# MLP opening: eight weight blocks in buffers of their own, all twelve written ahead of the first product; early rows for the odd layer's output projection; a weight ring of nine

## The chip, the cores and the metric

The kernel runs on one core of a Trainium2 chip. The metric is the device time of one execution in microseconds (us), the median of three runs. In the profile the engines are PE (matrix multiply), DVE (vector), ACT (scalar), POOL (general) and SP, which issues the transfers.

## The reference

A trunk of two mixer layers, each followed by a squared-ReLU MLP, and a final normalisation. Input and output are 1024 tokens of 1024 channels in float32; the hidden width of an MLP is 4096.

```python
def sq_relu_mlp(h, w1, w2):
    u = jax.nn.relu(h @ w1)
    return (u * u) @ w2
...
def odd_mixer(h, w_in, ..., w_out):
    ...
    yc = dense_mla(qn, qr, kn, rope(kr), v)      # 8 heads, all keys, softmax
    yd = rglru_block(xr, xg, ...)                # recurrent branch
    return jnp.concatenate([yc, yd], axis=-1) @ w_out
```

Every layer is `x + layer(rmsnorm(x))`: even mixer (windowed attention beside a pooling branch), MLP 0, odd mixer, MLP 1, final norm.

## The kernel before, in words

Activations lie channel-major, 128 channels by 1024 tokens to a tile (`N2` = 512 is half the tokens). To keep float32 accuracy every operand of a product is split into a rounded high part and the rest: `split` is a cast, usually on ACT (L122), and a subtraction on DVE or POOL (L130). A product then takes three matrix multiplies, high by high, high by low, low by high (`mm3`, L185).

**The MLPs** use a seven-product scheme for 2x2 blocks. For each pair of hidden blocks `p` the first matrix gives the weight blocks A11, A12, A22 and the sums S1 to S4 (formed on POOL); the input gives B11 and B21 (the first half of the tokens) and t2, t3, T1, t4, B22, which mix both halves. One product (L378) is 12 matrix multiplies of 128x512: four channel blocks by three. `w_stream` is a generator that loads raw blocks (`raw`, 128x1024, 512 KB), splits the wanted block (`prep`, under high priority) and yields it; `Ahead` keeps some blocks of it made in advance, and `take` hands them out. The split blocks (`wb`) come from the ring of `W_BUFS` buffers tagged "w"; the other large tiles (`raw`, `hb` for split inputs, X) come from the pool `G` of 41.

An MLP **opens** with the pairs 0 to 5 (`NS` = 6), for which it runs A11·B11 (`head`, whose result ACT copies to `t1`, L396) and A12·B21 (`head2`, into the same PSUM tile, so it has to wait for that copy): 12 products that need only the first half of the tokens. Meanwhile the second half is finished: the sum of squares goes through PE (`ss`, L220), the reciprocal root through ACT and DVE, PE spreads it over the partitions (`rb`, L231), ACT copies it to `RB` (L235). Then `late` makes the mixed inputs, on DVE eight scaled halves (L1528), four differences (L1540), the t2, t3, T1 and t4 combinations (L1543 to L1555) and twenty splits with their casts on ACT. The **rest** of each opening pair needs those.

**The odd layer's end.** Eight heads of attention run in 128 steps `u`: scores, exponentials (ACT), their scaling (`e`, L1106, POOL), transposes (`ctp`, L1350) copied to `cpT` (ACT L1353, DVE L1354), and values (`cav`, L1124), which lag by `ODD_LAG` = 4 steps. The recurrent half `yd` is done long before. After the last step the output projection (`op`, L185) runs over two token halves `n` and eight blocks `m`, each with eight channel blocks `k`, the `yd` half (k 4 to 7) first. Its weights go through `fetch`: a raw ring of two, a transfer of 512 KB, a cast on ACT, a subtraction on POOL (`wl`, L130), both into the "w" ring. Its results close the layer's norm and open MLP 1, so the last of them and the first products of the MLP are interleaved.

The order on each engine is set by a scheduler that goes by priorities and free buffers when the program is built; at run time each engine works through its list in that order.

Of the kernel before, what the change touches and what calls it, by code (L numbers as in the profile page):

```python
# [10 lines left out]
F32R = mybir.dt.float32r  # L11
# [13 lines left out]
N2 = 512  # L25
# [21 lines left out]
class Trunk:  # L47
# [89 lines left out]
    def requests(self, ph):  # L137
        a = self.a
        if ph == "even":
            r = [(a["e_w_in"][i], S) for i in (4, 5, 0, 1, 2, 3)] + [(a["e_w_pool"], N2)]  # L140
            r += [(a["e_w_in"][i], S) for i in (9, 8, 7, 6)]
            r += [(a["e_w_out"][1][m], S, "act", "pool") for m in range(4)]
            return r + [(a["e_w_out"][0][m], S) for m in range(4)]
        if ph == "odd":
            idx = {"xr3": 6, "ckv": 2, "cq0": 0, "cq1": 1, "xg0": 7, "xg1": 8, "xg2": 9, "xg3": 10}
            late = {"kn": (a["w_uk"], N2), "qr": (a["w_uq_r"], N2), "qn": (a["w_uq_n"], S), "vn": (a["w_uv"], N2)}
            r = [(a["o_w_in"][i], S, "act" if i != 5 else "pool") for i in (3, 4, 5)]
            seen = set()
            for op in ODD_START:
                k = op[:-1]  # L150
                if k in seen:
                    continue
                seen.add(k)
                if k in idx:
                    r.append((a["o_w_in"][idx[k]], S, "pool"))
                elif k in late:
                    r.append(late[k])
            return r + [(a["o_w_out"][m], S, "act", "pool") for m in range(NC)] * 2
        if ph == "final":
            return []  # L160
        l = int(ph[-1])
        return [(a["w2"][l, f], S) for p in TAIL for f in pair(p)]
# [5 lines left out]
    def fetch(self, ahead):  # L168

        while self.wreq and len(self.wout) < ahead:  # L170
            src, n, *eng = self.wreq.pop(0)
            raw = self.wp.tile([P, S], F32, tag="raw", name=self.nm("raw"), bufs=RAW_BUFS)
            self.nc.sync.dma_start(raw[:, :n], src)
            h = self.wp.tile([P, S], F32R, tag="w", name=self.nm("wh"))
            l = self.wp.tile([P, S], F32R, tag="w", name=self.nm("wl"))
            self.split(h[:, :n], l[:, :n], raw[:, :n], *eng)
            self.wout.append((h, l))

# [93 lines left out]
    def block(self, tag, x, le="dve", neg=False):  # L272

        nc = self.nc
        w = self.wp.tile([P, S], F32R, tag="w", name=self.nm(tag)) if tag == "wb" else self.G(tag, F32R)
        h, l = w[:, :N2], w[:, N2:]
        if neg:
            nc.scalar.activation(h, x, AF.Copy, scale=-1.0)
# [11 lines left out]
    def w_stream(self, l, order, second, look=0):  # L290
# [23 lines left out]
            sums[p, b] = self.H2("sum", "sum")  # L314
            return sums[p, b]

        def prep(p, b):
            if b in ("A11", "A12", "A22"):
                x = blk(p, int(b[1]) - 1, int(b[2]) - 1)
            elif b == "S1":  # L320
# [12 lines left out]
            else:  # L333
# [6 lines left out]
                else:  # L340
                    x = sums[p, "S2"]
                    add(x, x, blk(p, 0, 1), op=ALU.add)
            return self.block("wb", x)

        uses = {"A11": (0,), "A12": (1,) if second else (0,), "A22": (1,), "S1": (0, 1) if second else (1,),
                "S2": (0, 1), "S3": (0,) if second else (0, 1), "S4": (0, 1)}
        for k, (p, b) in enumerate(order):
            for q, c in order[k:k + look + 1]:
                for i in uses[c]:
                    raw(q, i)  # L350
            with self.tc.high_priority():
                w = prep(p, b)
            yield w

    def first_stream(self, l):
# [7 lines left out]
    def mlp(self, l, nb, nxt, dram):  # L363
# [5 lines left out]
        stream = nb.stream  # L369
# [547 lines left out]
    def odd(self, nb, xs, nxt):  # L917
# [195 lines left out]
        def av(u):  # L1113
# [13 lines left out]
            if p % 2 == 1 and kk == 3:  # L1127
                if h % 2 == 0 and p == 1:
# [4 lines left out]
                nc.vector.tensor_tensor(yc[h // 2][r:r + 64, (p // 2) * N2:(p // 2 + 1) * N2], ACC[0][0:64],  # L1133
                                        tmp[0:64], op=ALU.add)

        prep = iter(())
        for u in range(4 * NS):
            i, kk = divmod(u, 4)
            h, p = steps[i]
            for op in ODD_STEP:  # L1140
# [11 lines left out]
                elif op == "V":  # L1152
                    av(u - ODD_LAG)
                elif op == "P":
                    if p == 0 and kk == 0 and 1 <= h < 7:
                        prep = prep_qk(h + 1)
                    next(prep, None)
            if p == 1 and kk == 3 and h < 7:
                VS[h + 1] = self.head_values(h + 1, Vn)
        Yh, Yl = [None] * 8, [None] * 8  # L1160
        for c in range(4):
            Yh[4 + c], Yl[4 + c] = self.G("yh", F32R), self.G("yl", F32R)
            for s in H2:
                self.split(Yh[4 + c][:, s], Yl[4 + c][:, s], yd[c][:, s], "act", "pool")
# [10 lines left out]
        for n in range(2):  # L1175
            for m0 in range(0, NC, 2):
                W = [self.weight(), self.weight()]
                grp = [(m0 + j, self.PS("op")) for j in range(2)]
                for part in range(2):
                    ks = order[4 * part:4 * part + 4]  # L1180
                    for m, ps in grp:
                        w = W[m - m0]
# [131 lines left out]

    def head_values(self, h, Vn):
        nc = self.nc
        VS = self.wp.tile([P, S], F32R, tag="w", name=self.nm("VS"))
        vv = VS.rearrange("p (b t d) -> p b t d", b=8, t=2)
        for i in range(4):
            src = Vn[i].rearrange("p (b h d) -> p b h d", b=2, h=8)[:, :, h, :]  # L1320
# [23 lines left out]
    def mla_transpose(self, pr, kk):  # L1344
        nc = self.nc
        tp = self.PB("ctp")
        for i in range(2):
            for j in range(2):
                kb = 2 * kk + i
                nc.tensor.transpose(tp[:, (2 * i + j) * P:(2 * i + j + 1) * P], pr[j][:, kb * P:(kb + 1) * P],  # L1350
                                    self.ident)
        pp = self.wp.tile([P, S], F32R, tag="w", name=self.nm("cpT"))
        nc.scalar.copy(pp[:, :N2], tp)  # L1353
        nc.vector.tensor_tensor(pp[:, N2:], tp, pp[:, :N2], op=ALU.subtract)  # L1354
        return pp
# [324 lines left out]
LOOK = 7  # L1680

G_BUFS = 41
W_BUFS = 8
RAW_BUFS = 2


# [125 lines left out]
```

## Time and profile before

| | |
|---|---|
| median of 3 runs | 2158.83 us (2158.75 to 2159.36) |
| profiled execution, device time | 2161.66 us |
| its span, first to last instruction | 2159.5 us |
| PE busy | 2051.3 us, 95% of the span |
| DVE / ACT / POOL busy | 1542.9 / 1065.0 / 823.2 us |
| mean granted PE clock | 0.987 |
| opening of MLP 0 / MLP 1, first product to fifteenth | 311 to 373 / 1484 to 1544 us |
| last steps of the odd attention | 1379 to 1403 us |

A timeline row reads: start, duration, engine, line, operation, output <- inputs, count, and in brackets the idle time before it on its engine with what ended that. Matrix multiplies overlap, so a row of 60 in 13.89 us means 0.2315 us for each.

### The profile page before, as it was taken

To read this page: it belongs to the slowest core of one execution; us is meant where nothing else is said; L and a number is where in the kernel's file an instruction comes from. 1 tells how busy PE (TensorE), PEld (TensorE's weight loads), DVE (VectorE), ACT (ScalarE), POOL (GpSimd) and SP (SyncE) were. 2 spreads that over 40 slices of the span, in tenths; PEclk is the share of its full clock that TensorE was granted. 3 is DMA by queue.
4 is the path that set the end of the run, shared out by engine and by line. 5 is a ranking of instruction groups with operands and counts; after the bars stand their busy time and mean duration, and the time that the engine had idled before them with its cause. 6 is when DMAs were issued, how large, how long until landed. Compare 5 with 4: busy or idle time off the path is not lost.

```text
span 2159.5 us, 27248 instructions
## 1 busy us (share of the span) xinstructions
PE 2051.3 (95%) x9600; PEld 1688.1 (78%) x9600; DVE 1542.9 (71%) x2365; ACT 1065.0 (49%) x1853; POOL 823.2 (38%) x635
## 2 busy tenths in 40 slices
PE   6989998999999999999997999999899999999997
PEld 5867776787777888888785898888678777788887
DVE  7688868765656877775898888717875655877964
ACT  5236645444544534340565777734645545544423
POOL 4133332332315142242557776463242321522414
PEclk9999999999999999999999999999999999999999
DMA  5630052543448535132102000245443445654302
GB/s 176 144 136 24 11 185 78 176 166 127 151 152 310 176 107 180 55 101 76 35 25 68 11 11 10 79 130 188 135 172 127 152 155 179 236 204 157 127 29 79
DMA packets 115544, 261.32 MB, mean 121 GB/s; under 512 B 19664, under 2 KB 21840, under 8 KB 115408
## 3 DMA queue, kind: packets, MB, share of 16 engines
q1 hardware_dynamic: 115408, 259.59, 35.7%
q8 instruction: 75, 1.23, 0.2%
q14 instruction: 61, 0.50, 0.1%
HBM read 178.28 MB, written 72.35 MB: 116 GB/s over the span
## 4 chain that ended last, share of the span: by engine, by line
PE 72%; DVE 12%; issue 5%; ACT 5%; DMA 3%; POOL 3%; SPq 0%; POOLq 0%; DVEq 0%; ACTq 0%
PE q L498 22%; PE q L378 22%; PE op L185 7%; PE z L185 6%; PE ms L1334 4%; PE o L185 3%; PE cav L1124 2%; PE ctp L1350 2%; DVE th L1443 1%; POOL acc L245 1%; DVE wb L130 1%; DMA X<-xm 1%; DMA raw<-in_e_w_in_dram 1%; PE tp L870 1%; DVE w L1433 0%
## 5 line engine op out<-in xcount | busy, mean ns | idle before, releaser
L378 PE MATMUL q<-hb,wb 128*128 128x512 f32 x2688 | 629.7, 394 | 34.6 <-DVE wb L130 9.8
L378 PEld LDWEIGHTS q<-hb,wb 128*128 128x128 f32 x2688 | 504.1, 189 | 158.2 <-DVE wb L130 12.8
L498 PE MATMUL q<-ub,wb 128*128 128x512 f32 x2352 | 539.3, 391 | 8.8 <-ACT wb L122 7.0
L498 PEld LDWEIGHTS q<-ub,wb 128*128 128x128 f32 x2352 | 443.2, 189 | 104.3 <-ACT wb L122 8.8
L130 DVE TENSOR_TENSOR wb<-raw,wb 128x512 fp32r<-128x512 f32 x268 | 226.6, 851 | 112.6 <-ACT wb L122 112.2
L122 ACT CAST wb<-raw 128x512 fp32r<-128x512 f32 x268 | 164.3, 619 | 183.0 <-PE q L378 112.7
L122 ACT CAST wb<-sum 128x512 fp32r<-128x512 f32 x152 | 93.8, 620 | 183.3 <-PE q L378 100.7
L130 DVE TENSOR_TENSOR ub<-ut,ub 128x512 fp32r<-128x512 f32 x168 | 136.3, 824 | 66.2 <-ACT ub L122 65.8
L122 ACT CAST ub<-ut 128x512 fp32r<-128x512 f32 x168 | 101.4, 618 | 147.2 <-DVE wb L130 18.8
L130 DVE TENSOR_TENSOR wb<-sum,wb 128x512 fp32r<-128x512 f32 x152 | 126.3, 833 | 22.5 <-ACT wb L122 21.5
L185 PE MATMUL z<-Hh,wh 128*128 128x512 f32 x328 | 129.8, 400 | 10.6 <-ACT wh L122 9.6
L245 POOL TENSOR_TENSOR acc<-acc,sq 128x512 f32<-128x512 f32 (+1 forms) x62 | 88.3, 1427 | 123.3 <-ACT sq L244 121.4
L185 PE MATMUL z<-Hl,wh 128*128 128x512 f32 x328 | 130.2, 397 | 4.1 <-DVE Hl L1471 4.0
L185 PE MATMUL z<-Hh,wl 128*128 128x512 f32 x328 | 129.1, 394 | 0.8 <-DVE wl L130 0.8
L323 POOL TENSOR_TENSOR sum<-raw,raw 128x512 f32<-128x512 f32 x28 | 40.3, 1448 | 215.6 <-DMA raw<-in_w_dram 184.4
L332 POOL TENSOR_TENSOR raw<-raw,raw 128x512 f32<-128x512 f32 x32 | 43.5, 1360 | 203.2 <-DVE wb L130 175.6
L1124 PE MATMUL cav<-cpT,VS 128*128 128x256 f32 x512 | 102.7, 305 | 3.6 <-ACT cpT L1353 2.3
L122 ACT CAST wh<-raw 128x1024 fp32r<-128x1024 f32 (+1 forms) x49 | 49.8, 1015 | 111.9 <-PE z L185 39.4
L1334 PE MATMUL ms<-Kt,Qt 128*128 128x512 f32 (+1 forms) x384 | 99.8, 396 | 2.2 <-ACT e L1341 1.4
L185 PE MATMUL op<-yh,wh 128*128 128x512 f32 x252 | 100.0, 398 | 1.4 <-DVE ya L887 0.9
L185 PE MATMUL op<-yl,wh 128*128 128x512 f32 x252 | 98.9, 393 | 0.0
L185 PE MATMUL op<-yh,wl 128*128 128x512 f32 x252 | 98.0, 393 | 0.0
(343 smaller groups left out, 3815.0 us busy)
## 6 DMA issues: line engine op xcount, KB each, us to landing
raw<-in_w_dram SPq DMA_DIRECT2D x140, 512.0 KB, 4.5
xm<-X SPq DMA_DIRECT2D x32, 256.0 KB, 2.0
X<-xm SPq DMA_DIRECT2D x16, 512.0 KB, 6.6
raw<-in_o_w_out_dram SPq DMA_DIRECT2D x16, 512.0 KB, 3.5
raw<-in_o_w_in_dram SPq DMA_DIRECT2D x11, 512.0 KB, 3.5
raw<-in_e_w_in_dram SPq DMA_DIRECT2D x10, 512.0 KB, 5.1
X<-in_x_dram SPq DMA_DIRECT2D x16, 256.0 KB, 5.6
raw<-in_e_w_out_dram SPq DMA_DIRECT2D x8, 512.0 KB, 3.6
```

The costliest lines, as they stand in the source:

```text
L122: self.nc.scalar.copy(out, x)
L130: e.tensor_tensor(out, x, y, op=ALU.subtract)
L185: self.nc.tensor.matmul(ps, l, r, start=(first and i == 0), stop=(last and i == n - 1))
L245: (eng or nc.gpsimd).tensor_tensor(acc, acc, sq, op=ALU.add)
L323: add(x, blk(p, 1, 0), blk(p, 1, 1), op=ALU.add)
L332: add(x, x, blk(p, 1, 0), op=ALU.add)
L378: nc.tensor.matmul(ps, a, b, start=(first and c == 0 and i == 0), stop=(c == 3 and i == 2), skip_group_check=True)
L498: nc.tensor.matmul(ps[m], a, b, start=(first and j == 0 and i == 0), stop=(j == len(pairs) - 1 and i == 2), skip_group_check=True)
L870: nc.tensor.transpose(tp[:, h * P:(h + 1) * P], pt[h // 2][:, o:o + P], self.ident)
L1124: nc.tensor.matmul(ACC[0][:, (p % 2) * 256:(p % 2 + 1) * 256], VS[h][:, kb * P:(kb + 1) * P], pp[:, t * N2 + ii * 256:t * N2 + (ii + 1) * ...
L1334: nc.tensor.matmul(ps[:, s], l[rows, qs], r[rows, s], start=(i == 0), stop=(i == 2))
L1350: nc.tensor.transpose(tp[:, (2 * i + j) * P:(2 * i + j + 1) * P], pr[j][:, kb * P:(kb + 1) * P], self.ident)
```

## The change

Three things are changed. (1) In the first matrix of an MLP, blocks 4 to 11 of the opening get tiles of the pool `G`, tagged `ws`, instead of places in the "w" ring; all twelve opening blocks are written out (`stream.fill(2 * NS)`) ahead of the first product; and the raw loads look only two blocks ahead there. (2) The splits of `yd` move from after the attention into the steps 96 to 111; the `yd` halves of the output weights of m = 0 to 3 are loaded as half tiles (`owr`) and split (`ow`) in steps 105 to 117; and the 48 matrix multiplies of those halves for n = 0 (`out_early`) are written out from step 120 on, between transposes and values. The later loop leaves them out, and its first four weight requests load half the width. (3) `W_BUFS` goes from 8 to 9; the raw ring stays at 2.

```diff
-            return r + [(a["o_w_out"][m], S, "act", "pool") for m in range(NC)] * 2
+            return r + [(a["o_w_out"][m][:, :N2], N2, "act", "pool") for m in range(4)] + \
+                [(a["o_w_out"][m], S, "act", "pool") for m in [*range(4, NC), *range(NC)]]
...
-        w = self.wp.tile([P, S], F32R, tag="w", name=self.nm(tag)) if tag == "wb" else self.G(tag, F32R)
+        w = self.wp.tile([P, S], F32R, tag="w", name=self.nm(tag), bufs=W_BUFS) if tag == "wb" else self.G(tag, F32R)
...
-            return self.block("wb", x)
+            return self.block("ws" if own else "wb", x)
...
         for k, (p, b) in enumerate(order):
-            for q, c in order[k:k + look + 1]:
+            own = not second and 4 <= k < 2 * NS
+            for q, c in order[k:k + (2 if k < 2 * NS and not second else look) + 1]:
...
-                w = prep(p, b)
+                w = prep(p, b, own)
...
         early = {}
+        stream.fill(2 * NS)
         for p in start:
...
+        def out_early():
+            two = [self.PS2("op"), self.PS2("op")]
+            for m in range(4):
+                w = early[m][0]
+                ps = two[m // 2][:, (m % 2) * N2:(m % 2 + 1) * N2]
+                early[m].append(ps)
+                for k in range(4):
+                    cs, lo = slice(k * P, (k + 1) * P), slice(N2 + k * P, N2 + (k + 1) * P)
+                    self.mm3(ps, [(w[:, cs], w[:, lo], Yh[4 + k][:, H2[0]], Yl[4 + k][:, H2[0]])], k == 0, False)
+                    if k % 2:
+                        yield
...
+                    if 96 <= u < 112 and u % 2 == 0:
+                        y_split((u - 96) // 4, H2[u // 2 % 2])
+                    if 104 <= u < 120 and u % 4 == 1:
+                        out_weights((u - 104) // 4)
+                    if u >= 120:
+                        next(fill, None)
...
-                for part in range(2):
+                ready = n == 0 and m0 < 4
+                grp = [(m0 + j, early[m0 + j][1] if ready else self.PS("op")) for j in range(2)]
+                for part in range(1 if ready else 0, 2):
...
-W_BUFS = 8
+W_BUFS = 9
```

How the scheduler's order moves is shown at three places. First PE in the opening of MLP 1, around `ss` (the row with `ones`) and `rb` (the row with `ident`). Before:

```order
4521 L378 MATMUL q_13056<-hb_12906,wb_12890 128x512 x3
4522 L378 MATMUL q_13113<-hb_12816,wb_12898 128x512 x3
4523 L378 MATMUL q_13113<-hb_12820,wb_12898 128x512 x3
4524 L378 MATMUL q_13113<-hb_12902,wb_12898 128x512 x3
4525 L378 MATMUL q_13113<-hb_12906,wb_12898 128x512
4526 L220 MATMUL ss_13039<-ones,acc_12701 128x1 x4
4527 L378 MATMUL q_13014<-hb_12927,wb_12895 128x512 x3
4528 L378 MATMUL q_13014<-hb_12986,wb_12895 128x512 x3
4529 L378 MATMUL q_13014<-hb_13007,wb_12895 128x512 x3
4530 L378 MATMUL q_13014<-hb_13011,wb_12895 128x512 x3
4531 L378 MATMUL q_13113<-hb_12906,wb_12898 128x512 x2
4532 L231 MATMUL q_13056<-ident,rr_13054 128x128 x4
```

Now:

```order
4532 L380 MATMUL q_13090<-hb_13020,ws_13027 128x512 x3
4533 L380 MATMUL q_13090<-hb_13024,ws_13027 128x512 x3
4534 L380 MATMUL q_13235<-hb_12833,ws_13040 128x512 x3
4535 L380 MATMUL q_13235<-hb_12837,ws_13040 128x512 x3
4536 L380 MATMUL q_13235<-hb_12916,ws_13040 128x512 x3
4537 L380 MATMUL q_13235<-hb_12920,ws_13040 128x512 x3
4538 L221 MATMUL q_13059<-ones,acc_12718 128x1 x4
4539 L380 MATMUL q_13059<-hb_12941,wb_12907 128x512 x3
4540 L380 MATMUL q_13059<-hb_12999,wb_12907 128x512 x3
4541 L380 MATMUL q_13059<-hb_13020,wb_12907 128x512 x3
4542 L380 MATMUL q_13059<-hb_13024,wb_12907 128x512 x3
4543 L232 MATMUL rb_13105<-ident,rr_13088 128x128 x4
```

Before, 34 matrix multiplies of products stand ahead of `ss`; now 72 do, six whole products, two of them with `ws` blocks next to it. After `rb` comes a product into q_13142, which holds an A11·B11 result that ACT has to copy first.

Second ACT at the same place, from the copy to `RB` on (L235 before, L236 now). `hb` casts of `t` are the first split mixed inputs (t2); COPY `t` <- `q` is `head`'s copy. Before:

```order
1187 L235 COPY RB_12364<-q_13056 128x512
1188 L122 CAST wb_13115<-raw_12883 128x512
1189 L122 CAST wb_13139<-raw_12893 128x512
1190 L401 ACTIVATE t_2319_13057<-q_13056 128x512
1191 L402 ACTIVATE t_2319_13057<-t_2319_13057 128x512
1192 L122 CAST hb_13084<-t_2321_13082 128x512
1193 L122 CAST hb_13110<-t_2321_13082 128x512
1194 L396 COPY t_2326_13114<-q_13113 128x512
```

Now:

```order
1194 L403 ACTIVATE t_2322_13060<-q_13059 128x512
1195 L404 ACTIVATE t_2322_13060<-t_2322_13060 128x512
1196 L236 COPY RB_12432<-rb_13105 128x512
1197 L122 CAST hb_13116<-t_2331_13114 128x512
1198 L122 CAST hb_13139<-t_2331_13114 128x512
1199 L398 COPY t_2335_13143<-q_13142 128x512
1200 L122 CAST hb_13162<-t_2336_13160 128x512
1201 L122 CAST hb_13185<-t_2336_13160 128x512
1202 L398 COPY t_2340_13189<-q_13188 128x512
```

The weight casts have left this stretch. The copy of q_13142 stands behind the first two casts of t2, that of q_13188 behind the next two. In the opening of MLP 0 the same copies stand behind the same casts.

Third PE in the last steps of the odd attention. Before:

```order
4091 L1350 MATMUL ctp_12205<-ident,e_12029 128x128
4092 L1350 MATMUL ctp_12205<-ident,e_12069 128x128
4093 L1124 MATMUL cav_12240<-cpT_12186,VS_11843 128x256 x3
4094 L1124 MATMUL cav_12240<-cpT_12198,VS_11843 128x256
4095 L1350 MATMUL ctp_12217<-ident,e_12029 128x128
4096 L1350 MATMUL ctp_12217<-ident,e_12069 128x128
```

Now:

```order
4099 L1127 MATMUL cav_12160<-cpT_12176,VS_11855 128x256
4100 L186 MATMUL op_12224<-yh_11864,ow_12078 128x512
4101 L186 MATMUL op_12224<-yh_11959,ow_12078 128x512
4102 L186 MATMUL op_12224<-yl_11960,ow_12078 128x512
4103 L1386 MATMUL ctp_12211<-ident,e_11975 128x128
4104 L1386 MATMUL ctp_12211<-ident,e_12022 128x128
```

Multiplies of the output projection now stand inside the steps; of the last eight steps five have none.

More of the change, by code (lines that the diff above doesn't have):

```diff
@@ L173, in fetch @@
             self.nc.sync.dma_start(raw[:, :n], src)
-            h = self.wp.tile([P, S], F32R, tag="w", name=self.nm("wh"))
-            l = self.wp.tile([P, S], F32R, tag="w", name=self.nm("wl"))
+            h = self.wp.tile([P, S], F32R, tag="w", name=self.nm("wh"), bufs=W_BUFS)
+            l = self.wp.tile([P, S], F32R, tag="w", name=self.nm("wl"), bufs=W_BUFS)
             self.split(h[:, :n], l[:, :n], raw[:, :n], *eng)
@@ L315, in tmp, with prep @@
             return sums[p, b]
-        def prep(p, b):
+        def prep(p, b, own):
             if b in ("A11", "A12", "A22"):
@@ L1134, in av, with y_split, out_weights @@
                                         tmp[0:64], op=ALU.add)
+        Yh, Yl = [None] * 8, [None] * 8
+        early = {}
+        def y_split(c, s):
+            if s.start == 0:
+                Yh[4 + c], Yl[4 + c] = self.G("yh", F32R), self.G("yl", F32R)
+            self.split(Yh[4 + c][:, s], Yl[4 + c][:, s], yd[c][:, s], "act", "pool")
+        def out_weights(m):
+            raw = self.H2("owr", "owr")
+            dma(raw, a["o_w_out"][m][:, N2:])
+            w = self.G("ow", F32R)
+            self.split(w[:, :N2], w[:, N2:], raw, "act", "pool")
+            early[m] = [w]
+        def out_early():
[9 more added lines that the diff above has]
+                        yield
+        fill = out_early()
         prep = iter(())
@@ L1159, in odd @@
                 VS[h + 1] = self.head_values(h + 1, Vn)
[L1160 to L1164, printed above, removed]
         X = self.load_x(xs)
@@ L1167, in odd @@
             av(u)
+        for _ in fill:
+            pass
         for k in range(4):
@@ L1177, in odd @@
                 W = [self.weight(), self.weight()]
-                grp = [(m0 + j, self.PS("op")) for j in range(2)]
-                for part in range(2):
+                ready = n == 0 and m0 < 4
+                grp = [(m0 + j, early[m0 + j][1] if ready else self.PS("op")) for j in range(2)]
+                for part in range(1 if ready else 0, 2):
                     ks = order[4 * part:4 * part + 4]
@@ L1316, in head_values @@
         nc = self.nc
-        VS = self.wp.tile([P, S], F32R, tag="w", name=self.nm("VS"))
+        VS = self.wp.tile([P, S], F32R, tag="w", name=self.nm("VS"), bufs=W_BUFS)
         vv = VS.rearrange("p (b t d) -> p b t d", b=8, t=2)
@@ L1351, in mla_transpose @@
                                     self.ident)
-        pp = self.wp.tile([P, S], F32R, tag="w", name=self.nm("cpT"))
+        pp = self.wp.tile([P, S], F32R, tag="w", name=self.nm("cpT"), bufs=W_BUFS)
         nc.scalar.copy(pp[:, :N2], tp)
```

## The prediction

> **What bounds the kernel now.** I read the page first, then PE's timeline with its waits at the three places the change touches, then DVE, ACT and POOL there.
>
> ```profile
> PE 2051.3 (95%) x9600; PEld 1688.1 (78%) x9600; DVE 1542.9 (71%) x2365; ACT 1065.0 (49%) x1853; POOL 823.2 (38%) x635
> ...
> L378 PE MATMUL q<-hb,wb 128*128 128x512 f32 x2688 | 629.7, 394 | 34.6 <-DVE wb L130 9.8
> ...
> L498 PE MATMUL q<-ub,wb 128*128 128x512 f32 x2352 | 539.3, 391 | 8.8 <-ACT wb L122 7.0
> ```
>
> PE is the bound, and the change gives it the same multiplies in another order: it can win only idle or slow PE time. The first matrix of both MLPs loses 34.6 us to waits, the second 8.8. In the opening of MLP 1, PE did this:
>
> ```profile
> 1492.57 7.42 PE L378 MATMUL q<-hb,wb 128*128 128x512 f32 x32
> 1499.83 0.95 PE L220 MATMUL ss<-ones,acc 128*128 128x1 f32 x8
> ...
> 1503.95 1.05 PE L231 MATMUL q<-ident,rr 128*128 128x128 f32 x8
> 1505.43 6.00 PE L378 MATMUL q<-hb,wb 128*128 128x512 f32 x24 [0.42 <-ACT wb L122]
> 1512.14 0.73 PE L378 MATMUL q<-hb,wb 128*128 128x512 f32 x2 [0.71 <-ACT wb L122]
> 1515.47 6.86 PE L378 MATMUL q<-hb,wb 128*128 128x512 f32 x22 [2.59 <-DVE wb L130]
> 1523.75 5.76 PE L378 MATMUL q<-hb,wb 128*128 128x512 f32 x24 [1.41 <-ACT t L396]
> 1529.92 13.89 PE L378 MATMUL q<-hb,wb 128*128 128x512 f32 x60 [0.41 <-ACT t L396]
> 1544.31 13.84 PE L378 MATMUL q<-hb,wb 128*128 128x512 f32 x60 [0.50 <-DVE u L410]
> ...
> 1574.59 14.34 PE L378 MATMUL q<-hb,wb 128*128 128x512 f32 x62 [1.41 <-DVE u L410]
> ```
>
> 60 multiplies take 13.89 us, 0.2315 each, a product of 12 takes 2.78. The tenth product ends at 1529.9, the fifteenth at 1543.8. The waits up to there sum to 5.5 us; the 22 after 2.59 us of idling took 6.86 us instead of 5.1, 1.8 us of slow clock. What sets the later work is the late chain behind `rb`:
>
> ```profile
> 1506.42 5.39 DVE L1528 SCALAR_TENSOR_TENSOR X<-X,cols,RB 128x512 f32<-128x512 f32 x8 [0.32 <-ACT RB L235]
> ...
> 1526.18 6.09 DVE L130 TENSOR_TENSOR hb<-X,hb 128x512 fp32r<-128x512 f32 x10
> ...
> 1526.16 3.23 ACT L122 CAST hb<-X 128x512 fp32r<-128x512 f32 x6
> 1529.28 0.58 ACT L396 COPY t<-q 128x512 f32<-128x512 f32 x1
> ```
>
> The eight scalings take 5.3 us, other DVE operations 0.61 each, casts 0.54, a copy 0.58. The last row is the point: a copy that PE needs stood behind six casts that it has nothing to do with.
>
> **MLP 1's opening, costed.** Count multiplies from the moment when 48 of the projection are left. Before, 48 + 34 = 82 come ahead of `ss`, which ran at 1499.8. Now 48 + 72 = 120 do, since eight weight blocks more are ready and the scheduler puts six whole products there. 38 x 0.2315 = 8.8 us: `ss` at 1508.6 by the old clock. The eight added `ws` splits, 8 x 0.61 = 4.9 us on DVE, lie under PE's 28 us there. After `ss` (0.8) and one product (2.8) `rb` runs at 1512.2 to 1513.1. From `rb` to the first scaling went 2.5 us before; ACT has two activations to do first again, and I take 1.7: 1513.9, against 1506.4. The late chain starts 7.5 us later. Four weight splits (4 x 0.61) no longer stand in it, which gives 2.4 back.
>
> PE's next row after `rb` is a product into q_13142, which waits for a copy that stands on ACT behind the first two casts of t2. Those need eight scalings (5.3), four differences (2.4) and three combinations (1.8): 1523.4; then a cast and the copy, 1524.6. PE idles 11.5 us, where before it had three products to run. Then 2.8 us and 1.8 of slow clock to 1529.2; the next copy, behind two casts more, is ready at 1529.4; a third at 1532.0. So the tenth product ends at 1535, the wait for t2's weight split costs 1, and five more products (13.9) end at 1549.4, against 1543.8: **+5.6**. It is a DVE bound, so no row behind it gives the time back.
>
> **MLP 0's opening.**
>
> ```profile
> 317.67 10.59 PE L378 MATMUL q<-hb,wb 128*128 128x512 f32 x46
> 328.11 0.95 PE L220 MATMUL ss<-ones,acc 128*128 128x1 f32 x8
> ...
> 330.69 4.14 PE L378 MATMUL q<-hb,wb 128*128 128x512 f32 x10 [0.98 <-DVE wb L130]
> 334.67 1.05 PE L231 MATMUL q<-ident,rr 128*128 128x128 f32 x8
> ...
> 344.22 6.92 PE L378 MATMUL q<-hb,wb 128*128 128x512 f32 x22 [3.37 <-DVE wb L130]
> ...
> 359.26 13.89 PE L378 MATMUL q<-hb,wb 128*128 128x512 f32 x60 [0.41 <-ACT t L396]
> ...
> 336.37 5.39 DVE L1528 SCALAR_TENSOR_TENSOR X<-X,cols,RB 128x512 f32<-128x512 f32 x8
> ```
>
> Here the weight waits (0.98, 3.37) were real, and they go: six products run through from 317.7 to 334.4, where before it was four. But `rb` now follows `ss` with nothing between: 2.4 us for the root, 1.3 idle, `rb` at 336.8, first scaling at 338.5, 2.1 later than 336.4. The seventh product ends at 341.3; then PE waits for the copy behind t2's casts, 338.5 + 5.3 + 2.4 + 1.8 + 0.6 + 0.6 = 349.2, 7.9 us idle. With the slow clock and the next copies the eleventh ends at 363.3, the fifteenth at 374.4, against 373.2: **+1.2**. The stalls don't go, they gather in one place.
>
> **The drain.**
>
> ```profile
> 1383.54 0.36 PE L1124 MATMUL cav<-cpT,VS 128*128 128x256 f32 x1 [1.37 <-ACT cpT L1353]
> 1383.74 0.60 PE L1350 MATMUL ctp<-ident,e 128*128 128x128 f32 x4
> ...
> 1386.42 0.60 PE L1350 MATMUL ctp<-ident,e 128*128 128x128 f32 x4
> ...
> 1387.94 0.60 PE L1350 MATMUL ctp<-ident,e 128*128 128x128 f32 x4
> ...
> 1391.45 0.60 PE L1350 MATMUL ctp<-ident,e 128*128 128x128 f32 x4
> ...
> 1392.36 0.60 PE L1350 MATMUL ctp<-ident,e 128*128 128x128 f32 x4
> ...
> 1395.71 0.99 PE L1124 MATMUL cav<-cpT,VS 128*128 128x256 f32 x4 [1.02 <-DVE cpT L1354]
> ...
> 1401.33 0.60 PE L1350 MATMUL ctp<-ident,e 128*128 128x128 f32 x4
> ...
> 1390.00:1400.00 10.00, 8.24 (x52) 7.27 (x52) 9.34 (x14) 7.87 (x15) 3.30 (x3) 0.83 0.90 357
> ```
>
> An unhindered step takes 0.91 us (1391.45 to 1392.36); a step short of its copy 1.52 (1386.42 to 1387.94). Twelve steps from 1383.74 to 1401.33 took 17.6 us instead of 10.9; with the 1.37 ahead of them 8.1 us are to be won, of which the slow clock (0.83 in that window) makes about 1.7. Covered steps run at PE's pace. Five of the last eight have nothing in them: 5 x 0.6 = 3.0 stay. Then new waits come, because 48 multiplies (11.1 us) that covered the next weights have been used:
>
> ```profile
> L130 POOL TENSOR_TENSOR wl<-raw,wh 128x1024 fp32r<-128x1024 f32 x14 | 35.3, 2524 | 42.5 <-ACT wh L122 42.5
> ...
> L122 ACT CAST wh<-raw 128x1024 fp32r<-128x1024 f32 (+1 forms) x49 | 49.8, 1015 | 111.9 <-PE z L185 39.4
> ...
> raw<-in_o_w_out_dram SPq DMA_DIRECT2D x12, 512.0 KB, 3.6
> ...
> L1106 POOL TENSOR_SCALAR e<-e,csm 128x1024 f32<-128x1024 f32 x28 | 31.5, 1125 | 39.9 <-DVE csm L1105 34.6 <-PE ctp L1350 2.9 <-DVE cnb L1339 2.2
> ...
> L130 POOL TENSOR_TENSOR yl<-th,yh 128x512 fp32r<-128x512 f32 x2 | 2.5, 1282 | 0.0
> ...
> 315.24 5.10 POOL L245 TENSOR_TENSOR acc<-acc,sq 128x512 f32<-128x512 f32 x1 [8.46 <-ACT sq L244]
> ```
>
> The half weight of m = 2 is cast behind the last `cpT` copy and split on POOL (1.28): 0.7 us. Its PSUM tile makes the next row wait for the addition to X: 1.0. The weight of m = 4 is requested only when that split frees its raw buffer: 3.6 to land, 1.0 for the cast, 2.5 for the split, 7.1 against 26 multiplies and that 1.0, 7.0 us: 0.1. So 8.1 - 3.0 - 1.8 = 3.3: **-3.3**. The bounds: -8.1 if nothing stays, +1 if the weight chain stalls for a second pair (3.6). The twelve added POOL operations (eight splits moved, four new), 12 x 1.28 = 15.4 us, fit into the 39.9 us that POOL idled ahead of its scalings; the twelve casts, 12 x 0.54 = 6.5 us, lie beside PE's work of those 24 steps. The four half transfers replace half of four that stand later on SP. If that cover failed, the scalings would be late: the third rival.
>
> [...]
>
> **The ring of nine** and the shifts elsewhere. The first DVE and ACT rows, the even layer and the second matrices change by a place or two. A gain would show at weight-buffer waits: 7.0 us on L498, and 9.8 - 0.98 - 3.37 - 2.59 = 2.9 on L378 outside the openings. But at 674.99 the cast was late for this reason:
>
> ```profile
> 673.69 0.62 ACT L122 CAST ub<-ut 128x512 fp32r<-128x512 f32 x1 [5.65 <-DMA ut<-ut_3T]
> ```
>
> It stood behind a cast that waited for a load of stored results, which a ninth buffer does not hasten, and ACT's order there is unchanged. I take 0, between -9.9 and +2.
>
> **The sum**: 1.2 + 5.6 - 3.3 + 0 = +3.5. Against the profiled execution, 2161.66, that is 2165.2; the median of the runs is 2.83 lower, so 2158.8 + 3.5 = 2162.3. No change and a change can't be told apart within 0.2%, 4.3 us: the forecast lies just inside, on the slow side.
>
> **Rivals.** (a) Faster: the ninth buffer is what the late casts lack. All 9.9 us above go, and the sum is -6.4: 2152.4. It decides from 7.8 us on. For it: the waits name weight casts; against it: the row above. (b) The openings are not later, because PE's spare time behind them absorbs it (waits for DVE such as the 0.50 and 1.41 in the first timeline): at most 3 us in each, and the sum is -2.5: 2156.3, no change. Against it: those waits are chains from PE's own products and shift with them. (c) Slower: POOL's moved splits meet a busy DVE. At the 5.10 us of the `acc` row the twelve cost 61 us, over the 39.9 that are free by 21; the lag of four steps hides a part, I take half: 2172. It decides from 3.4 us each. For it: DVE is busy 9.34 of 10 us in the window row of the drain; against it: POOL's subtractions in the same steps took 1282 ns. [...]
>
> **How the numbers follow.** Forecast 0.55, its own range 2158 to 2167, of which 0.31 within the bound and 0.24 slower; (a) 0.16; (b) 0.14; (c) 0.15. That gives faster 0.16, same 0.45, slower 0.39. The range leaves out half of (a) and half of (c): 2152.4 to 2171.
>
> **What would show it.** `ss` of MLP 1 after 72 multiplies of products, the first late scaling 7 us further behind the projection's end, then a PE wait of 10 to 12 us for a copy of `t`; one of about 8 in MLP 0 and no weight waits of 0.98 or 3.37; attention steps at PE's pace with a few waits at the end and at m = 2 and 4. Wrong would be: the waits for `t` under 5 us, the fifteenth product no later, or L498's waits gone.

## The result, and the profile after

The changed kernel takes 2182.36 us (median of 4 runs, 2180.79 to 2183.74) against 2159.1: a ratio of 1.0105 (95% interval 1.0089 to 1.0121), 23 us slower. The forecast was 2162.3, with a range up to 2171.0.

The page of the changed kernel, engines and the two product lines:

```profile
PE 2054.4 (94%) x9600; PEld 1693.8 (78%) x9600; DVE 1553.0 (71%) x2365; ACT 1057.1 (49%) x1857; POOL 822.5 (38%) x639
...
L380 PE MATMUL q<-hb,wb 128*128 128x512 f32 x2496 | 584.3, 394 | 33.0 <-ACT t L398 16.2
L501 PE MATMUL q<-ub,wb 128*128 128x512 f32 x2352 | 538.4, 390 | 10.2 <-ACT wb L122 5.8
```

PE does the same work, 3 us longer, and the rest of the loss is idling. The second matrix (L501) is as before. In the first matrix the waits changed their name, from DVE's weight splits to ACT's copy of `t`, as forecast. The openings look much as forecast; PE's timeline in MLP 0, then MLP 1:

```profile
337.85 2.05 PE L232 MATMUL q<-ident,rr 128*128 128x128 f32 x8 [3.61 <-DVE rr L212]
340.57 5.49 PE L380 MATMUL q<-hb,ws 128*128 128x512 f32 x12 [0.68 <-ACT RB L236]
351.35 5.49 PE L380 MATMUL q<-hb,ws 128*128 128x512 f32 x12 [5.29 <-ACT t L398]
...
1517.89 1.05 PE L232 MATMUL rb<-ident,rr 128*128 128x128 f32 x8
1530.65 10.56 PE L380 MATMUL q<-hb,ws 128*128 128x512 f32 x36 [11.71 <-ACT t L398]
```

The 0.98 and 3.37 of weight waits are gone; MLP 0 waits 5.29 us for the copy of `t` (forecast 7.9), MLP 1 has one wait of 11.71 (forecast 11.5). The drain too: PE full and at full clock, then two small waits, 0.29 us for the split of m = 2's weight (forecast 0.7) and 1.19 behind m = 2 for the addition to X (forecast 1.0). The first row is a window: its length, the busy time of PE, PE's weight loads, DVE, ACT and POOL, the granted clock, and DMA's share and GB/s. The second is PE's timeline:

```profile
1388.00:1423.40 35.40, 35.38 (x219) 30.91 (x217) 21.19 (x37) 19.95 (x36) 8.03 (x7) 1.00 0.35 134
...
1427.47 0.47 PE L186 MATMUL op<-yh,wh 128*128 128x512 f32 x1 [1.19 <-DVE X L1222]
```

What the forecast looked at only for weight-buffer waits is the rest of the first matrix, pairs 6 to 15. PE's timeline there, MLP 0, before:

```profile
479.09 39.00 PE L378 MATMUL q<-hb,wb 128*128 128x512 f32 x168 [0.79 <-DVE t L407]
518.87 38.97 PE L378 MATMUL q<-hb,wb 128*128 128x512 f32 x168 [0.78 <-DVE t L407]
558.62 39.00 PE L378 MATMUL q<-hb,wb 128*128 128x512 f32 x168 [0.78 <-DVE t L407]
```

and after:

```profile
522.23 3.02 PE L380 MATMUL q<-hb,wb 128*128 128x512 f32 x12 [2.64 <-ACT t L398]
525.95 35.80 PE L380 MATMUL q<-hb,wb 128*128 128x512 f32 x156 [0.71 <-ACT wb L122]
564.44 4.61 PE L380 MATMUL q<-hb,wb 128*128 128x512 f32 x12 [2.68 <-ACT t L398]
569.75 35.84 PE L380 MATMUL q<-hb,wb 128*128 128x512 f32 x156 [0.71 <-ACT wb L122]
608.23 4.36 PE L380 MATMUL q<-hb,wb 128*128 128x512 f32 x12 [2.64 <-ACT t L398]
```

168 multiplies are two pairs. Before, such a double pair took 39.8 us with one wait of 0.78; now 42.2 (522.23 to 564.44) or 43.8 (to 608.23), with 2.64 + 0.71 of waiting and, in the longer ones, 12 multiplies at 4.4 to 4.6 us in place of 2.8 (granted clock 0.64 from 564.4 to 569.1, 0.66 from 608.23 to 612.6). Both MLPs show it.

### The profile page after: what moved, and what is told of

Same layout as the page of the kernel before. It is cut to its first block, busy times and chain, and to the rows that moved or that the text cites. A ratio compares the mean times of both kernels' runs of the same rounds, so it can differ in the third digit from the quotient of the medians.

```text
span 2178.8 us, 27258 instructions
## 1 busy us (share of the span) xinstructions
PE 2054.4 (94%) x9600; PEld 1693.8 (78%) x9600; DVE 1553.0 (71%) x2365; ACT 1057.1 (49%) x1857; POOL 822.5 (38%) x639
## 4 chain that ended last, share of the span: by engine, by line
PE 73%; DVE 10%; issue 7%; ACT 4%; DMA 3%; POOL 3%; SPq 0%; POOLq 0%; DVEq 0%; ACTq 0%
PE q L501 22%; PE q L380 20%; PE z L186 7%; PE op L186 6%; PE o L186 4%; PE ms L1370 4%; PE cav L1127 3%; PE ctp L1386 2%; DVE wb L130 2%; PE gt L186 1%; POOL acc L246 1%; PE tp L873 1%; ACT wb L122 1%; DMA raw<-in_w_dram 1%; DVE X L1564 1%
## 5 line engine op out<-in xcount | busy, mean ns | idle before, releaser
L380 PE MATMUL q<-hb,wb 128*128 128x512 f32 x2496 | 584.3, 394 | 33.0 <-ACT t L398 16.2
L380 PEld LDWEIGHTS q<-hb,wb 128*128 128x128 f32 x2496 | 469.4, 189 | 145.8 <-ACT t L398 21.7
L501 PE MATMUL q<-ub,wb 128*128 128x512 f32 x2352 | 538.4, 390 | 10.2 <-ACT wb L122 5.8
L501 PEld LDWEIGHTS q<-ub,wb 128*128 128x128 f32 x2352 | 441.9, 188 | 106.0 <-ACT wb L122 7.5
L130 DVE TENSOR_TENSOR wb<-raw,wb 128x512 fp32r<-128x512 f32 x252 | 230.1, 917 | 77.6 <-ACT wb L122 77.4
L122 ACT CAST wb<-raw 128x512 fp32r<-128x512 f32 x252 | 154.7, 618 | 173.7 <-PE q L380 96.4
L130 DVE TENSOR_TENSOR ub<-ut,ub 128x512 fp32r<-128x512 f32 x168 | 135.2, 816 | 60.1 <-ACT ub L122 59.3
L130 DVE TENSOR_TENSOR wb<-sum,wb 128x512 fp32r<-128x512 f32 x152 | 135.9, 897 | 58.5 <-ACT wb L122 57.9
L343 POOL TENSOR_TENSOR sum<-sum,raw 128x512 f32<-128x512 f32 x32 | 43.1, 1346 | 186.2 <-DVE wb L130 186.2
L1390 DVE TENSOR_TENSOR cpT<-ctp,cpT 128x512 fp32r<-128x512 f32 x128 | 87.1, 687 | 16.5 <-ACT cpT L1389 14.3
L1389 ACT CAST cpT<-ctp 128x512 fp32r<-128x512 f32 x128 | 74.2, 586 | 39.6 <-PE ctp L1386 39.0
```

The lines of the kernel that those rows point to most:

```text
L122: self.nc.scalar.copy(out, x)
L130: e.tensor_tensor(out, x, y, op=ALU.subtract)
L380: nc.tensor.matmul(ps, a, b, start=(first and c == 0 and i == 0), stop=(c == 3 and i == 2), skip_group_check=True)
L501: nc.tensor.matmul(ps[m], a, b, start=(first and j == 0 and i == 0), stop=(j == len(pairs) - 1 and i == 2), skip_group_check=True)
```

## The experiments

**Which part costs what.** Four kernels take the change apart.

e1, the changed kernel with the ring of eight:

```diff
-W_BUFS = 9
+W_BUFS = 8
```

> The changed kernel with the ring of eight restored; own tiles and early rows stay. Theory A: the ninth buffer lets the scheduler put the next pair's A11.B11 product ahead of A12.B21 in the pairs 6 to 15 of both MLPs, and the weight splits ahead of a subtraction on DVE; that costs 8.7 and 8.1 us there. Then the double pairs go back from 42.2 and 43.8 us to 39.8, the waits of 2.6 us for the copy of t go, and the time falls by 16.8, less about 4 us that the ninth buffer may have given in the attention: about 2169.5 (2165 to 2173). Theory B: the own tiles and the short look ahead of the opening shift the stream of raw blocks for the rest of the loop, and the ring has no part: 2180 to 2187 with the waits still there.

e2, the kernel before with `W_BUFS = 9` alone.

> The kernel before with the ring of nine and nothing else. Theory A (the ring reorders the loop of the pairs 6 to 15): the waits of 2.6 us for the copy of t appear in both MLPs, +17, and the attention gains about 4: about 2172 (2167 to 2176). Theory B (the opening's own tiles do it): no such waits, 2153 to 2160.

e3, the kernel before with the own tiles, the twelve blocks ahead and the shorter lookahead alone (the diff's lines of `w_stream` and `stream.fill(2 * NS)`).

> The kernel before with the opening's own tiles and all twelve blocks written ahead, ring of eight, no early rows. By the prediction's working the openings cost 1.2 and 5.6 us: 2165.9; by the changed kernel's trace 2.2 and about 6: about 2167 (2163 to 2169). Rival: what the openings lose is taken up behind them, 2158 to 2161. Theory B of the loop would give 2175 or more.

e4, the kernel before with the early rows alone (the diff's lines of `requests`, `y_split`, `out_weights`, `out_early`).

> The kernel before with the early rows of the output projection alone, ring of eight, opening as before. By the prediction's working 3.3 us are won: 2155.8; by the changed kernel's trace, where the steps from 112 on and the last waits gained more, 5 to 8: about 2153 (2150 to 2157). Rival: the weights of m = 2 and 4 or POOL take it back, 2158 to 2162.

| | median, us | ratio to before | 95% interval |
|---|---|---|---|
| after | 2182.36 | 1.0105 | 1.0089 to 1.0121 |
| e1, ring of eight | 2167.32 | 1.0034 | 1.0021 to 1.0047 |
| e2, ring of nine alone | 2182.90 | 1.0100 | 1.0084 to 1.0116 |
| e3, own tiles alone | 2179.00 | 1.0085 | 1.0071 to 1.0098 |
| e4, early rows alone | 2162.59 | 1.0013 | 1.0004 to 1.0022 |

By stretches, from the start times of PE's rows in each profiled execution, as the difference to before in us (products are counted in groups of 12 multiplies; the attention is counted from its first transpose; the 48 early multiplies, 11.1 us, are put back where they stood before). The profiled executions took 2161.66 us before and 2180.79 after, so the columns don't add up to the differences of the medians:

| stretch | before | after | e1 | e2 | e3 | e4 |
|---|---|---|---|---|---|---|
| to MLP 0's first product | 311.2 | +0.9 | +1.0 | +2.9 | -1.7 | -1.7 |
| to its 15th | 62.5 | +2.2 | +2.7 | -0.8 | +2.8 | 0.0 |
| to its 56th | 116.5 | +1.5 | +4.0 | +0.8 | +3.9 | 0.0 |
| pairs 6 to 15 on, to the second matrix | 157.6 | +8.7 | -0.1 | +9.0 | -0.1 | -0.1 |
| second matrix and start of the odd layer | 540.2 | +3.0 | +0.3 | +6.0 | +2.9 | -0.5 |
| attention, to the last `cav` | 219.9 | -11.8 | -4.0 | -5.5 | +0.8 | -3.7 |
| to MLP 1's 15th product | 136.5 | +7.2 | +7.3 | +0.9 | +7.0 | +8.1 |
| to its 56th | 117.5 | -0.5 | -2.5 | +1.7 | +3.0 | 0.0 |
| pairs 6 to 15 on, to the second matrix | 158.7 | +7.7 | -0.1 | +6.2 | -0.1 | -1.3 |
| to PE's last row | 330.9 | +1.4 | +0.6 | +2.0 | -0.7 | +1.0 |

Theory A holds for the loop: the ring of nine costs 8.7 + 7.7 us there with the rest of the change and 9.0 + 6.2 without it, and with eight buffers the loop is as before. e2 missed its number (2172 expected) mainly because the ring also delays the odd layer's start by 6 us, as much as it gains in the attention, and MLP 0's first product by 2.9. e3 came out 12 us dearer than expected, and parts that cost +19.4 and +3.0 alone cost +7.7 together: they don't add, as the stretch to MLP 1's 15th product shows (7.0, 8.1, and 7.3 for both).

**Why the loop waits.** DVE in the changed kernel ahead of the wait that ended at 522.23, and POOL in the same stretch:

```profile
513.76 0.69 DVE L130 TENSOR_TENSOR wb<-sum,wb 128x512 fp32r<-128x512 f32 x1 [1.58 <-ACT wb L122]
514.37 0.68 DVE L421 TENSOR_TENSOR u<-q,t 128x512 f32<-128x512 f32 x1
514.97 1.41 DVE L130 TENSOR_TENSOR wb<-raw,wb 128x512 fp32r<-128x512 f32 x1
516.31 1.78 DVE L130 TENSOR_TENSOR wb<-sum,wb 128x512 fp32r<-128x512 f32 x1
518.01 1.77 DVE L130 TENSOR_TENSOR wb<-raw,wb 128x512 fp32r<-128x512 f32 x1
519.71 0.67 DVE L426 TENSOR_TENSOR t<-t,q 128x512 f32<-128x512 f32 x1
```

```profile
514.54 1.29 POOL L343 TENSOR_TENSOR sum<-sum,raw 128x512 f32<-128x512 f32 x1 [8.64 <-DVE wb L130]
515.79 1.75 POOL L328 TENSOR_TENSOR sum<-raw 128x512 f32<-128x512 f32 x1
517.61 1.62 POOL L329 TENSOR_TENSOR sum<-sum,raw 128x512 f32<-128x512 f32 x1
```

PE waits for ACT's copy of `t`; the copy stands behind two activations of the previous pair's `t`; these wait for L426, and L426 stands behind three weight splits. These three splits and POOL's three additions take turns: POOL's first ends at 515.83, the split 0.55 later; POOL's next, listed from 515.79, ends 1.2 us after that, the next split 0.55 later, and so on. The splits come out 3 us late in sum, PE's wait is 2.64. One pair later the same three splits stand in the same place, and POOL is idle until 546.80; there each takes 0.69 us, and PE does not wait:

```profile
543.03 0.69 DVE L130 TENSOR_TENSOR wb<-raw,wb 128x512 fp32r<-128x512 f32 x1
543.64 0.69 DVE L130 TENSOR_TENSOR wb<-sum,wb 128x512 fp32r<-128x512 f32 x1
545.98 0.69 DVE L130 TENSOR_TENSOR wb<-raw,wb 128x512 fp32r<-128x512 f32 x1 [1.65 <-ACT wb L122]
...
546.80 1.28 POOL L333 TENSOR_TENSOR raw<-raw,raw 128x512 f32<-128x512 f32 x1 [11.63 <-issue]
```

With nine buffers weights are cast earlier, so three splits stand there in both pairs; with eight it was three in one pair and one in the other, the one beside POOL. Two kernels test this.

e5 holds one of the nine buffers during pairs 6 to 15:

```diff
+        held = self.wp.tile([P, S], F32, tag="w", name=self.nm("held"), bufs=W_BUFS)
+        self.pin(V.memset(held[:, :8], 0.0))
         for p in range(NS, NP):
...
+        self.pin(V.tensor_copy(self.small("free", 8), held[:, :8]))
```

> The changed kernel whole, with the ring of nine, but one of the nine buffers is held by an unused tile from the first pair 6 to the end of each first matrix, so that the pairs 6 to 15 run on eight. Theory A (the depth of the ring in these pairs sets their order, and the order the waits): the waits of 2.6 us for the copy of t go in both MLPs, the double pairs take 39.8 us, and the attention keeps what the ninth buffer gave: 2182.4 - 16.3 = 2166 (2163 to 2169). Rival (the rows differ for another reason, as the places of tiles in memory): the waits stay, 2178 to 2184.

e6 leaves POOL's sums of these pairs out, all but 8 of their 512 columns, so its result is no longer that of the MLP:

```diff
...
+            w = N2 if second or at[0] < NS or at[0] >= NF // 2 else 8
+            if w == 8 and out is not x:
+                nc.gpsimd.memset(out, 0.0)
+            nc.gpsimd.tensor_tensor(out[:, :w], x[:, :w], y[:, :w], op=op)
...
```

> The changed kernel with POOL's work for the pairs 6 to 15 left out: the sums S1 to S4 of the first matrix are not formed (8 columns and a fill in place of 512-column additions). The order on PE and DVE stays that of the changed kernel, three weight splits ahead of the subtraction from t. Theory C: these splits are late only because they run beside POOL's additions, 1.4 to 1.8 us each in place of 0.6, 3.1 us together. Then they take 0.7 each, the waits of 2.6 us for the copy of t fall under 0.5 and the time to about 2168 (2165 to 2172). Rival: the order alone makes the wait, and it stays at 2 us or more: 2179 to 2184.

e6 took 2159.71 us (ratio 0.9997, 0.9988 to 1.0006), faster than expected: the waits for `t` are gone, and the whole gain lies in these stretches, which are now 2.6 and 3.6 us shorter than before the change. PE in e6:

```profile
520.74 38.71 PE L388 MATMUL q<-hb,wb 128*128 128x512 f32 x168 [0.71 <-ACT wb L122]
560.16 38.71 PE L388 MATMUL q<-hb,wb 128*128 128x512 f32 x168 [0.71 <-ACT wb L122]
```

Against its expectation the order on DVE moved as well: two of the three splits now stand ahead of L421 (L429 in e6). So e6 shows what the sums and this order cost together, and not which of the two it is.

e5 took 2174.57 (1.0072, 1.0059 to 1.0085), half of what was expected, and its misses are the best evidence. In the double pairs DVE and ACT have the order of the kernel before, operation by operation, and still some double pairs wait 0.78 us for L409 and others 2.41. DVE ahead of a short one and of a long one, with POOL's row behind each:

```profile
1696.25 0.69 DVE L130 TENSOR_TENSOR wb<-raw,wb 128x512 fp32r<-128x512 f32 x1
1696.85 0.69 DVE L438 TENSOR_TENSOR T<-u,T 128x512 f32<-128x512 f32 x1
1697.98 0.69 DVE L409 TENSOR_TENSOR t<-q,t 128x512 f32<-128x512 f32 x1 [0.44 <-PE q L380]
...
1697.67 1.27 POOL L328 TENSOR_TENSOR sum<-raw 128x512 f32<-128x512 f32 x1 [9.35 <-DMA ut_8t<-T]
...
1736.02 1.78 DVE L130 TENSOR_TENSOR wb<-raw,wb 128x512 fp32r<-128x512 f32 x1
1737.71 1.75 DVE L438 TENSOR_TENSOR T<-u,T 128x512 f32<-128x512 f32 x1
1739.39 0.68 DVE L409 TENSOR_TENSOR t<-q,t 128x512 f32<-128x512 f32 x1
...
1735.63 1.61 POOL L328 TENSOR_TENSOR sum<-raw 128x512 f32<-128x512 f32 x1 [7.58 <-DVE T L434]
```

The same DVE rows in the same order: where POOL starts after them they take 0.69 us, where it starts 0.4 us ahead of them 1.78 and 1.75, and PE waits 1.6 us longer. So the order that the ring sets is only half the cause; what it does is to put DVE's splits beside POOL's sums. Theory C is shown, by these rows and by the two pairs of the changed kernel above; theory A in its first form (order alone) falls. In the long pair POOL had waited for a buffer that DVE's L434 releases; with eight buffers throughout the same additions follow at once on the one before (in the kernel before L327 is listed from 508.39, and the addition ahead of it ends at 508.42), and PE waits for L409 0.78 us each time (e1). Why the release comes so late in e5 is not settled; holding a buffer gives back 7.8 of the 15.0 us that e1 gives.

**Why the early rows give nothing.** e4 gains 3.7 us in the attention and loses 8.1 behind it, at a wait that the forecast had put down to the own tiles. PE in e4 (no own tiles):

```profile
1520.04 10.54 PE L379 MATMUL q<-hb,wb 128*128 128x512 f32 x36 [11.56 <-ACT t L397]
```

In e4, 31 multiplies of MLP 1's first products stand ahead of the projection's last 12 rows, where before it was 2. e7 adds an order edge from the projection's last row (`row`) to the six A11·B11 products:

```diff
...
+                    if behind and c == 0 and i == 0:
+                        self.tc.add_manual_dep(mm.ins, row, mybir.DependencyInfo(
+                            mybir.DependencyClass.NoSync, mybir.DependencyReason.DATA))
...
```

> The kernel before with the early rows of the output projection alone (2162.6 in this form, ring of eight), and one order edge more: the six A11.B11 products that open MLP 1 may not start ahead of the projection's last row. Theory D: the early rows are repaid because 31 multiplies of products now stand ahead of the projection's last 12 rows and hold the late chain up by 31 x 0.2315 = 7.2 us. Then the wait of 11.6 us for the copy of t shrinks to about 4 and the time is 2155.4 (2153 to 2158). Rival: the opening is bound by DVE's work on the first half, and the wait only moves: 2160 to 2164.

2167.90 (1.0036, 1.0023 to 1.0049): theory D falls. The wait for `t` shrank only to 8.92 us, and the rows now wait themselves:

```profile
1489.40 0.50 PE L186 MATMUL op<-yh,wh 128*128 128x512 f32 x1 [4.62 <-DVE X L1225]
```

e10 instead starts the first half's norm one output block sooner:

```diff
-        if c == 1:
+        at = c + self.l
+        if at == 1:
             self.sums(0)
...
```

> The kernel before with the early rows alone (2162.6, ring of eight), and in the odd layer's norm the first half's sums, factor and scaled inputs one output block sooner (behind the second half's blocks 0 and 1 in place of 1 and 2). Theory E: DVE idles until the first half's factor (RB at 1470.7) and is then full for 29 us, so that the additions to X of the last blocks stand in its queue; the early rows bring the projection forward but not that factor, which stands 44 multiplies behind its sums in place of 27. Moved, RB comes about 10 us sooner, DVE's work is done ahead of the last rows, and 6 to 9 us are won: 2155 (2151 to 2158). Rival: the weights of the output projection or the sums' own chain hold the rows: 2160 to 2164.

2162.15 (1.0014, 1.0005 to 1.0022): `RB` came at 1459.5 in place of 1470.7, but the wait stayed at 11.57. e12 is the same edit on the kernel before.

> The kernel before with the first half one block sooner and nothing else. Theory E: without the early rows the last additions to X stand only 0.4 to 2 us in DVE's queue, so little is won: 2156 to 2161. If the first half's time is worth something whatever the early rows do, it falls as much as with them, to 2153 or less.

2159.28 (1.0001, 0.9991 to 1.0011), no change. e16 makes both edits on e4; e17 also leads the edge to `ss`.

> The early rows alone with two edits at once: the edge that puts the projection's last rows ahead of MLP 1's products (2167.9 by itself, the rows then waited 4.62 us for an addition to X on DVE), and the first half one block sooner (2162.2 by itself, RB 11 us sooner, with 36 multiplies of products still ahead of the last rows). Theory E in its joint form: neither alone can help, because the one lacks DVE's time and the other PE's order. Together the rows run through, the projection ends 5 to 7 us sooner and so does the late chain: 2156 (2153 to 2159). If the late chain has another start, the wait for the copy of t only grows: 2161 or more.

> As e16, and one product alone stands between the projection's last row and the second half's sum (ss); the edge of the others leads to ss. 24 multiplies fewer, 5.6 us, stand ahead of it, of which the chain of addition, square and sum hides up to 2. By the joint theory E the late chain starts 3 to 5 us sooner still: 2152 (2149 to 2157). If DVE's own queue sets it: as e16.

e16: 2163.16 (1.0021, 1.0012 to 1.0030); e17: 2159.55 (1.0001, 0.9992 to 1.0010). PE in e16, then the waits for `t` in e17:

```profile
1478.44 0.50 PE L186 MATMUL op<-yh,wl 128*128 128x512 f32 x1 [3.35 <-POOL wl L130]
1488.86 0.50 PE L186 MATMUL op<-yh,wh 128*128 128x512 f32 x1 [0.78 <-DVE X L1225]
...
1517.17 4.26 PE L380 MATMUL q<-hb,wb 128*128 128x512 f32 x12 [3.39 <-ACT t L401]
1522.59 5.73 PE L380 MATMUL q<-hb,wb 128*128 128x512 f32 x24 [1.16 <-ACT t L401]
```

The joint theory misses both numbers. DVE's hold fell from 4.62 to 0.78, but 3.35 us for an output weight's split on POOL took its place, the wait for `t` stayed at 8.92 in e16, and e16 gained nothing. With `ss` ahead of the products the wait for `t` fell from 11.6 to 4.6 in sum, with 1.19 more ahead of `ss`. That is e4's loss undone at most, not more: e17 equals the kernel before, and the intervals of e4 and e17 still touch.

**Why the own tiles cost 19 us.** e9 writes out the six A11·B11 products first, so that their copies stand ahead of t2's casts on ACT:

```diff
         for p in start:
             ps = self.PS("q")
-            early[p] = (*head(p, ps), ps)
...
+            early[p] = (*head(p, ps, ready["A11", p]), ps)
+            if p == 1:
                 nb.sums(1)
...
+            if p == 2:
+                nb.factor(1)
+        for p in start:
+            next(late, None)
+            head2(p, early[p][2], early[p][1], ready["A12", p])
...
```

> The kernel before with the opening's own tiles (2179.0 in that form, ring of eight, no early rows), and the six A11.B11 products of an opening written out ahead of the six A12.B21 products and of the late inputs, so that all six copies of t stand on ACT ahead of the casts of t2. Theory F: the own tiles cost 6.8 us in MLP 0 and 10 in MLP 1 because these copies stand behind the casts and PE runs dry. Then the waits of 5.3 and 7.1 us for the copy go, with their slow clock, some 8 us in each MLP: 2163 (2157 to 2168). Rival: the late chain on DVE is the bound whatever PE does ahead of it, and the wait turns up at the first product with t2: 2175 to 2180.

2172.24 (1.0063, 1.0050 to 1.0076), 7 us better than e3, between the two expectations. The waits for `t` fell to 0.68; then PE ran dry at the first weight of the rest:

```profile
1544.93 15.42 PE L379 MATMUL q<-hb,wb 128*128 128x512 f32 x55 [14.01 <-ACT wb L122]
```

Its raw block had been asked for only at 1537. e13 adds `stream.fill()` behind the six products, e14 `stream.fill(p + 1)` behind each `head2`.

> The run before with six products first (own tiles, ring of eight, no early rows; 2172.2), and one line more: the next six weight blocks are written out right behind the six A11.B11 products, ahead of the late inputs. In that run PE ran dry for 16.2 us in MLP 0 and 14.0 in MLP 1 at the first product of the rest, for a weight cast behind a POOL sum whose raw blocks were asked for only at 1537, 5 us after the inputs t2 were ready (1532). Theory G: the opening's own tiles pay only if the rest's raw blocks are asked for ahead; then the waits shrink to 3 us or less and some 24 us go: 2148 (2144 to 2156). Rival H: the raw blocks can't come sooner because the eight own tiles hold places of the pool of 41 until their products have run: the waits stay at 10 us or more, 2165 to 2174.

> The same, but the next blocks are written out one by one, one behind each A12.B21 product. By theory G between the two: the raw blocks stand two transfers later in their queue, 2150 to 2160. By rival H as there, 2165 to 2174.

e13: 2180.65 (1.0094, 1.0080 to 1.0108); e14: 2173.03 (1.0055, 1.0042 to 1.0068). In e13 the raw blocks were asked for at 1523.7, and the wait fell apart without shrinking enough:

```profile
1541.02 13.68 PE L379 MATMUL q<-hb,wb 128*128 128x512 f32 x47 [5.09 <-DVE hb L130]
1557.15 12.76 PE L379 MATMUL q<-hb,wb 128*128 128x512 f32 x48 [2.46 <-ACT wb L122]
1575.52 5.03 PE L379 MATMUL q<-hb,wb 128*128 128x512 f32 x11 [5.61 <-DVE u L411]
```

Neither G nor H: the weights could come sooner, but PE then waits for DVE, for a late input's split (5.09) and later for a result `u` (5.61). The weights' splits stand in the same queue, and four DVE operations among the late inputs took 7.0 us together in place of 2.4 (from 1530.48: two of L1549 3.50, one of L1561 1.78, one of L130 1.75). These are the lengths that the loop shows beside POOL's additions; that POOL's four sums stand beside them here is an estimate from these lengths. The rest of the price of the own tiles, and why MLP 0 loses another 4 us between its 15th and 56th product with the ring of eight, was not settled.

**Combinations.** e8 (early rows, ring of nine with one buffer held, e7's edge), e11 (e1 with e9's and e10's edits) and e15 (e11 with e13's line):

> What the runs so far point to: early rows, ring of nine with one buffer held in the pairs 6 to 15, the order edge of the projection's rows, and the opening as before (no tiles of its own). If the ninth buffer's gain in the attention (7.8 us with the early rows) adds to theory D's 7.2: 2162.6 - 7.8 - 7.2 = 2147.6 (2145 to 2152). If the ring's price at the odd layer's start (3 to 6 us) comes with it: 2151 to 2154. If theory D fails: 2155 or more.

> The changed kernel with the ring of eight (2167.3 in that form) and both edits, heads first and the first half one block sooner. If theories E and F both hold: some 8 us from MLP 0's opening and 8 from MLP 1's: 2151 (2146 to 2157). If only F holds: 2159; if neither: 2165 or more.

> The changed kernel with the ring of eight, six products first, the first half one block sooner (2170.7 in that form), and the next six weight blocks ahead of the late inputs. By theory G 20 to 24 us less: 2148 (2144 to 2154). By rival H 2165 or more.

2177.63, 2170.65 and 2180.73: each ended in the branch that its expectation kept for failed theories, as D, E and G had failed singly and F had given 7 us of the 16 forecast. No version beats the kernel before.

## Why the prediction was wrong

- **The step that failed** is "The ring of nine and the shifts elsewhere": "I take 0, between -9.9 and +2". It weighs only weight-buffer waits that a ninth buffer could remove (2.9 us of them on L378 outside the openings) and puts a new order in the pairs 6 to 15 at nothing, though PE already waited 0.78 us for DVE there in each double pair. The runs show in its place: with nine buffers three weight splits stand ahead of L426 beside POOL's additions, they take 1.41 to 1.78 us in place of 0.69, and PE waits 2.64 + 0.71 us in each double pair, in some with slow clock behind it (0.64 from 564.4 to 569.1). That cost 8.7 + 7.7 = 16.4 us. Without the ninth buffer the kernel takes 2167.3 (e1), inside the range of 2152.4 to 2171.0 and 5 us above the forecast.
- The same step said that weight-cast waits of L498 would stay, since no buffer hastens them: right (7.0 before, 5.8 after, 6.4 in e2). Rival (a), which would remove them, fell.
- Within the step the attention was missed too: the ring alone wins 5.5 us there and pays 6.0 on the way to it.
- **MLP 1's opening**, +5.6: 11.71 us of waiting for 11.5, with the late chain's start and the copy behind t2's casts as forecast. Measured +7.2 with the early rows, +7.0 without. Part of the agreement is luck: the step gives the wait to the own tiles, but these alone make one of 7.11 (e3), and the early rows without them make one of 11.56 (e4). The step's own terms also end at 1549.9, not at 1549.4.
- **MLP 0's opening**, +1.2: +2.2 to the 15th product and +1.5 behind it. The idling ahead of `rb` was put at 1.3 us and took 3.61, with slow clock behind it (12 multiplies in 5.49 us, granted clock 0.50 from 340.57 to 346.06); the wait for `t` was put at 7.9 and took 5.29.
- **The drain**, -3.3: the steps gained 3.7 (e4), where -8.1 + 3.0 = -5.1 was forecast, and the waits at m = 2, behind it and at m = 4 took 0.27, 1.18 and none for 0.7, 1.0 and 0.1. But 8.1 us are given back between the attention's end and MLP 1's fifteenth product, where 1.8 was forecast. The sum treated drain and opening as two terms; the runs show that they draw on the same slack.
- Rival (c), POOL's moved splits beside a busy DVE, did not decide the drain. The same meeting of POOL and DVE decided the loop (splits of 1.41 to 1.78 us in place of 0.69), where nothing had been moved by hand.

## What to carry to other kernels

Where a scheduler sets the order, a buffer more is an edit of every loop that uses the ring: compare the order of the steady loop first, since a wait in it comes back with every turn (here 2.64 + 0.71 us in each double pair). Terms that draw on the same idle stretch don't add; cost them together. When a DVE operation on a chain has unsteady durations in the trace (here 0.69 and 1.78 us for the same split), lay POOL's rows beside it before looking for a late producer.

## What the runs showed of the hardware

In the loop a 128x512 operation on DVE with both inputs in SBUF took 0.69 us where POOL was idle (the splits from 543.03 of the changed kernel, L130 and L438 from 1696.25 of e5) and 1.41 to 1.78 beside POOL's additions (the splits from 514.97, e5's from 1736.02), each of these ending 0.55 us after a POOL operation ended; with an input from PSUM it stayed at 0.68 and 0.69 beside POOL (L421 at 514.37 with POOL's row from 514.54; L409 of e5 at 1697.98 with POOL's row from 1697.67). It is not always DVE that comes out late: in the kernel before, the addition on POOL that took 5.10 us from 315.24, where the same line took 1.29 from 305.49, met splits that DVE ran back to back at 0.68 each until 319.18; it ended 1.16 us after the last of them, and DVE's next split 0.55 after it. Why POOL's additions come between the splits in one place and not in the other is not shown.

The same PE wait was followed by full clock in one place and by slow clock in another: in the changed kernel 12 multiplies took 3.02 us after 2.64 of idling (granted clock 1.00 from 522.2 to 525.3), and 4.61 after 2.68 (0.64 from 564.4 to 569.1).
